# Two layer stacks on one core: SBUF tiles moved to multiples of 128 bytes, split weights 64 bytes past

## Chip, cores and metric

The kernel runs on one core of one Trainium2 chip. The time is that of one execution on the device in microseconds (us). Three timed runs of the kernel before have a median of 1580.65 us (1580.19 to 1584.49).

## What is computed

256 tokens of width 1024 pass through two layers and then a second block. Everything is float32.

```python
for i in range(2):                       # layers
    ff = swiglu(rms_norm(h, g[0]), w_gate_up[i, 0], w_down[i, 0]); h = h + 0.5 * rms_norm(ff, g[1])
    mix = short_conv_mixer(...) if i == 0 else gated_deltanet_mixer(...)   # on rms_norm(h, g[2])
    h = h + rms_norm(mix, g[3])
    ff = swiglu(rms_norm(h, g[4]), w_gate_up[i, 1], w_down[i, 1]); h = h + 0.5 * rms_norm(ff, g[5])
# second block: attention (three branches) beside an RWKV mixer, merged, and a convolved gated FFN
```

By far the most arithmetic is in the weight matrices: each of the four SwiGLUs multiplies by 1024 x 5632 and 2816 x 1024, the mixers by input and output projections, and the second block by the like. The recurrences, scores and norms are small beside them.

## The kernel before

**Weights.** All weight matrices are cut into tiles of 128 x 128 and laid in one stream (`wstream`) in the order of use, four tiles to a chunk of 128 x 512 floats. `Streamer` (line 620) brings each chunk by a DMA on the sync queue into one of six buffers `wraw`. ScalarE copies it, rounded, to a tile `whi` of type fp32r, and VectorE writes the difference `wraw - whi` to `wlo`; there are seven buffers of each. Twelve chunks are split ahead into room in the region `arG`.

**Products.** A weight product has 128 rows, 128 columns and 256 tokens. Its moving operand is split in the same way: `xh` and `xl` (1024 columns of the model in eight tiles of 256 tokens) for the up and input projections, tiles in the regions `a0`, `a1`, `a2` (all printed as `a`) for the down and output projections. `mm3` (line 794) issues three instructions for a tile: whi by the high part, whi by the low part, wlo by the high part. They sum into the same 256 columns of a PSUM bank. `mm3s` (line 801) does the same for a group of six column tiles, in the first two row tiles of a stage; on the first row tile it also multiplies by `x0`, the split update of the first tile (printed as `x`). The output of a column tile is complete after 8 row tiles (up) or 22 (down). Then VectorE and ScalarE take it from the bank.

**Order.** `Pace` (line 260) keeps an account of rough prices, makes a graph of all instructions and gives each engine a fixed order. It knows an operand by its tile's name and by the columns within the tile. Where in SBUF the tile lies isn't part of the account.

**Places.** Tiles are laid one behind another in each partition in the order of the calls `pool.tile`, each rounded up to 32 bytes. Before: `par` (2656 bytes), `con` (5888), `h`, `xh`, `xl`, `arM`, `fg`, `rb`, `rb2`, `acc` (all whole multiples of 128 long), `eps` (32), `half` (128), `tmp`, `stm` (whole multiples), five `pad` (1056 each), `x0`, `wraw`, `whi`, `wlo`, and then the regions `a0`, `a1`, `a2`, `arG`. The first starts at a multiple of 128. By these sums the starts modulo 128 bytes are:

| tiles | before | after |
|---|---|---|
| par | 0 | 0 |
| con, h, xh, xl, arM, fg, rb, rb2, acc | 96 | 0 |
| tmp, stm | 0 | 0 |
| pad0 to pad4 | 0, 32, 64, 96, 0 | 0, 32, 64, 96, 0 |
| x0 | 32 | 0 |
| wraw, whi, wlo | 32 | 64 |
| a0, a1, a2, arG | 32 | 0 |

Tiles inside these (the eight of xh, the four of a chunk, the slots of a) lie at whole multiples of 512 or 1024 bytes from the start.

The three products of a tile (lines 795 to 799):

```python
wh, wl = self.W.next()
nc.tensor.matmul(out, wh, xh, start=start, stop=False)
nc.tensor.matmul(out, wh, xl, start=False, stop=False)
nc.tensor.matmul(out, wl, xh, start=False, stop=stop)
```

Of the kernel before, what the change touches and what calls it, by code (L numbers as in the profile page):

```python
# [11 lines left out]
F32 = mybir.dt.float32  # L12
# [5 lines left out]
PSUM = bass.MemoryType.PSUM  # L18
# [28 lines left out]
class Product:  # L47
    """Tiles of one weight matrix in the order in which the tensor engine takes them: column tiles in
    groups, a group of several row tile by row tile, the columns beyond the groups one by one.
    A column tile is (weight, index, column ranges, row ranges of each row tile)."""  # L50
# [24 lines left out]
# The rule's input projection by column tile: queries 0-7, keys 8-15, values 16-31, output gates 32-47, and 48 for beta  # L75
# and the decay. The keys come first, whose inverse takes longest.
# [77 lines left out]
def low_rank(inputs):  # L154
    """The up projections of decay (with its bias as a row), learning rate and gate."""
    out = np.zeros((P, 1536), np.float32)
    out[:64, :512] = inputs["rwkv_w_up_2"][0]
    out[64, :512] = inputs["rwkv_w0_2"][0]
    out[64:, 512:1024] = inputs["rwkv_a_up_2"][0]
    out[:, 1024:] = inputs["rwkv_g_up_2"][0]  # L160
    return out


def cmp_w1(inputs):
    """Two tokens of a block, an even one and the next, over the partitions."""
# [4 lines left out]
def param_parts():  # L170
    """(name, columns, how the input is laid over 128 partitions)"""
# [66 lines left out]
class Staged:  # L238
    """Work on a sequence of items, whose later stages are issued with the next items' earlier ones."""
# [20 lines left out]
class Pace:  # L260
    """An account, by rough prices in us, of when each engine gets to what is issued to it and when each part of a
    tile was last written and read. Independent sequences of steps are interleaved by it."""
# [17 lines left out]
    def parts(self, ap):  # L280
        """The pieces of its tile that an access pattern touches."""
# [18 lines left out]
    def when(self, *aps):  # L300
        """When everything issued to these is done."""
# [20 lines left out]
    def columns(self, op, out, ins):  # L322
        """The columns for which a product holds the tensor engine, those that it counts, by its share of the rows, and
        the size of the square of the array that it takes."""
# [10 lines left out]
    def ranks(self):  # L335
        """Each instruction's place in the best of a few schedules. The first goes by the longest way to the end, and
        each other by the latest starts that the one before it leaves."""
# [27 lines left out]
    def schedule(self, order, before, after, forward):  # L365
        """Each instruction's start and end, where an engine that is free takes the first in this order of those that
        can start. The tensor engine runs at half its clock in a tick after one in which it was little used, and
        two products on the two halves of its columns go almost at once; so that it seldom is, products that use it
        little give way."""
# [76 lines left out]
    def arrange(self, tc, rank):  # L446
        """Has each engine take what was issued to it in the order of these ranks."""
# [8 lines left out]
    def node(self, engine, op, out, ins, outs, price):  # L456
        """An instruction of the graph, with those that come before it."""
# [132 lines left out]
class Chain:  # L590
    """A sequence of steps with the banks and buffers that it takes in turn."""
# [15 lines left out]
def alternate(*steps):  # L607
    """The sequences in turn, each waiting while another goes on."""
# [11 lines left out]
class Streamer:  # L620
    """Brings the weight tiles on chip ahead of their use, as high and low halves."""

    def __init__(self, K, n_raw=6, n_split=7):
        self.K = K
        self.nc = K.nc
        pool = K.pool
        self.raw = [pool.tile([P, CT * P], F32, name=f"wraw{i}") for i in range(n_raw)]
        self.hi = [pool.tile([P, ST * P], F32R, name=f"whi{i}") for i in range(n_split)]
        self.lo = [pool.tile([P, ST * P], F32R, name=f"wlo{i}") for i in range(n_split)]
# [1588 lines left out]
```

## Time and profile before

| what | value |
|---|---|
| median of three timed runs | 1580.65 us (1580.19 to 1584.49) |
| span of the profiled execution (its own time isn't recorded apart) | 1586.4 us |
| PE busy | 1569.7 us, 99%, 13,544 products |
| VectorE busy | 1202.2 us, 76% |
| ScalarE busy | 1026.9 us, 65% |
| DMA | 261.14 MB, mean 165 GB/s |

PE is TensorE's matrix product, PEld its loading of weights, DVE is VectorE, ACT is ScalarE, SP the sync queue. Every instruction of the program is issued through one helper, so all rows name the line L576, and they are told apart by the names of their tiles. A PE row's mean is the length of one product from start to end. As products are pipelined, the next one starts before the end, and the time from start to start is read from a timeline.

### The profile page before, as it was taken

How to read it: one execution, taken by the hardware profiler on the slowest of the kernel's cores; microseconds unless marked ns; L12 is line 12 of the kernel's file. 1: busy time of each engine (PE TensorE's matmuls, PEld its weight loads, DVE VectorE, ACT ScalarE, POOL GpSimd, SP SyncE). 2: the span in 40 equal slices, each digit the busy share in tenths (PEclk: the TensorE clock that was granted, in tenths of full speed). 3: DMA queues.
4: the chain of work that ended last, by engine and by line, in shares of the span. 5: the costliest groups of instructions: out<-in, count | busy, mean ns of one | idle time of the engine just before them, and what ended most of it. 6: DMA issues, size and time to landing. Idle time of an engine off the chain costs nothing.

```text
span 1586.4 us, 35927 instructions
## 1 busy us (share of the span) xinstructions
PE 1569.7 (99%) x13544; PEld 1517.6 (96%) x13544; DVE 1202.2 (76%) x2527; ACT 1026.9 (65%) x2153; POOL 10.4 (1%) x24
## 2 busy tenths in 40 slices
PE   9999999999999999999999999999999999999999
PEld 9999999999999999989898999999987877999999
DVE  7776597877658777689996778765887955889973
ACT  7555566765557557578887866555782766578763
POOL 0000000000000000000000000000010000000000
PEclk9999999999999999999999999999998989999999
DMA  8666556566665667525342456666533312566664
GB/s 275 192 186 187 180 176 186 170 190 187 184 185 167 201 193 245 180 79 168 116 138 81 135 159 201 187 187 184 168 106 101 120 35 87 172 187 188 187 194 118
DMA packets 142670, 261.14 MB, mean 165 GB/s; under 512 B 15904, under 2 KB 17952, under 8 KB 142368
## 3 DMA queue, kind: packets, MB, share of 16 engines
q1 hardware_dynamic: 142496, 258.84, 53.9%
q8 instruction: 106, 1.74, 0.4%
q14 instruction: 68, 0.56, 0.1%
HBM read 257.73 MB, written 1.05 MB: 163 GB/s over the span
## 4 chain that ended last, share of the span: by engine, by line
PE 93%; DVE 3%; ACT 2%; issue 1%; DMA 0%; SPq 0%; DVEq 0%
PE bank L576 93%; DVE a L576 1%; ACT a L576 1%; DVE wlo L576 1%; ACT stm L576 1%; DMA wraw<-wstream 0%; DVE arG L576 0%; ACT whi L576 0%; DVE stm L576 0%; ACT arG L576 0%; DVE fg L576 0%; DVE xl L576 0%; DVE tmp L576 0%; DVE acc L576 0%; ACT pad L576 0%
## 5 line engine op out<-in xcount | busy, mean ns | idle before, releaser
L576 ACT ACTIVATE whi<-wraw 128x512 fp32r<-128x512 f32 x956 | 599.3, 630 | 440.9 <-PE bank L576 335.5
L576 DVE TENSOR_TENSOR wlo<-wraw,whi 128x512 fp32r<-128x512 f32 x956 | 653.0, 688 | 291.2 <-ACT whi L576 282.6
L576 PE MATMUL bank<-xh,whi 128*128 128x256 f32 x2688 | 753.1, 284 | 6.1 <-DVE stm L576 3.6
L576 PE MATMUL bank<-xh,wlo 128*128 128x256 f32 x2688 | 751.6, 284 | 0.0
L576 PE MATMUL bank<-xl,whi 128*128 128x256 f32 x2688 | 745.7, 282 | 0.7 <-DVE xl L576 0.7
L576 PEld LDWEIGHTS bank<-xh,whi 128*128 128x128 f32 x2688 | 507.6, 190 | 15.2 <-issue 6.0
L576 PEld LDWEIGHTS bank<-xl,whi 128*128 128x128 f32 x2688 | 504.1, 189 | 8.8 <-issue 6.6
L576 PEld LDWEIGHTS bank<-xh,wlo 128*128 128x128 f32 x2688 | 502.0, 189 | 6.9 <-issue 6.0
L576 PE MATMUL bank<-a,whi 128*128 128x256 f32 x2272 | 411.0, 283 | 0.2
L576 PEld LDWEIGHTS bank<-a,whi 128*128 128x128 f32 x2272 | 353.6, 191 | 1.2 <-DVE a L576 0.4
L576 PE MATMUL bank<-a,wlo 128*128 128x256 f32 x1136 | 321.6, 283 | 0.0
L576 PEld LDWEIGHTS bank<-a,wlo 128*128 128x128 f32 x1136 | 217.2, 191 | 0.0
L576 DVE TENSOR_TENSOR tmp<-bank,rb 128x256 f32<-128x256 f32 x176 | 66.3, 418 | 8.0 <-ACT rb L576 0.6
L576 PE MATMUL bank<-a 64*128 64x256 f32 (+3 forms) x192 | 41.4, 397 | 1.4 <-DVE arG L576 1.4
L576 ACT ACTIVATE xh<-h,par 128x256 fp32r<-128x256 f32 x70 | 34.0, 498 | 12.0 <-DVE h L576 9.9
L576 ACT ACTIVATE arG<-bank 128x256 f32<-128x256 f32 (+2 forms) x87 | 37.8, 443 | 5.2 <-PE bank L576 4.9
L576 DVE SCALAR_TENSOR_TENSOR arG<-arG,par 128x256 f32<-128x256 f32 x88 | 40.0, 477 | 0.0
L576 ACT ACTIVATE a<-tmp 128x256 fp32r<-128x256 f32 x88 | 35.7, 406 | 6.5 <-DVE tmp L576 6.3
L576 DVE TENSOR_TENSOR acc<-acc,tmp 128x256 f32<-128x256 f32 x92 | 38.4, 418 | 2.0 <-ACT acc L576 0.9
L576 DVE TENSOR_TENSOR a<-tmp,a 128x256 fp32r<-128x256 f32 x88 | 36.7, 417 | 3.8 <-ACT a L576 3.8
L576 ACT ACTIVATE tmp<-tmp 128x256 f32<-128x256 f32 x88 | 35.4, 407 | 3.8 <-DVE tmp L576 3.7
L576 DVE TENSOR_TENSOR tmp<-tmp,tmp 128x256 f32<-128x256 f32 x88 | 36.7, 417 | 0.0
(253 smaller groups left out, 1229.5 us busy)
## 6 DMA issues: line engine op xcount, KB each, us to landing
wraw<-wstream SPq DMA_DIRECT2D x968, 256.0 KB, 2.8
arG<-cmp_w SPq DMA_DIRECT2D x1, 1024.0 KB, 4.7
out_dram<-h SPq DMA_DIRECT2D x8, 128.0 KB, 2.7
con<-consts SPq DMA_DIRECT2D x1, 734.0 KB, 4.7
h<-xt SPq DMA_DIRECT2D x1, 512.0 KB, 6.5
a<-lowrank SPq DMA_DIRECT2D x1, 512.0 KB, 4.0
par<-params SPq DMA_DIRECT2D x1, 283.5 KB, 4.8
h<-xt SPq DMA_DIRECT2D x2, 128.0 KB, 3.4
```

What stands on the lines that cost most here:

```text
L576: i = f(*args, **kw)
```

## The change

Only places change: the tiles `eps`, `half` and `pad` are allocated earlier, four filler tiles that nothing reads are added, and comments are gone. The sizes of the fillers (24, 32, 16 and 16 floats) bring the starts to the right column of the table above. No instruction, operand or order is changed.

```diff
 class Streamer:
     def __init__(self, K, n_raw=6, n_split=7):
         pool = K.pool
+        self.fill0 = pool.tile([P, 16], F32, name="fill2")
         self.raw = [pool.tile([P, CT * P], F32, name=f"wraw{i}") for i in range(n_raw)]
         self.hi = [pool.tile([P, ST * P], F32R, name=f"whi{i}") for i in range(n_split)]
         self.lo = [pool.tile([P, ST * P], F32R, name=f"wlo{i}") for i in range(n_split)]
+        self.fill1 = pool.tile([P, 16], F32, name="fill3")
...
+FILL = 24, 32
...
         self.par = pool.tile([P, N_PARAM], F32, name="par")
+        self.eps = pool.tile([P, 1], F32, name="eps")
+        self.half = pool.tile([P, 4, KD], F32, name="half")
+        self.pad = [pool.tile([P, T + 3], F32, name=f"pad{i}") for i in range(5)]
+        self.fill = [pool.tile([P, FILL[0]], F32, name="fill0")]
         self.con = pool.tile([P, N_CONST], F32, name="con")
+        self.fill += [pool.tile([P, FILL[1]], F32, name="fill1")]
         self.h = pool.tile([P, KD, T], F32, name="h")
...
-        self.eps = pool.tile([P, 1], F32, name="eps")
-        self.half = pool.tile([P, 4, KD], F32, name="half")
         self.tmp = [pool.tile([P, T], F32, name=f"tmp{i}") for i in range(8)]
         self.stm = [pool.tile([P, 512], F32, name=f"stm{i}") for i in range(4)]
-        self.pad = [pool.tile([P, T + 3], F32, name=f"pad{i}") for i in range(5)]
```

## Rows read from the trace of the kernel before

**Rows 1.** The page: busy time of each engine, and the chain that ended last.
```profile
PE 1569.7 (99%) x13544; PEld 1517.6 (96%) x13544; DVE 1202.2 (76%) x2527; ACT 1026.9 (65%) x2153; POOL 10.4 (1%) x24
...
PE 93%; DVE 3%; ACT 2%; issue 1%; DMA 0%; SPq 0%; DVEq 0%
```

**Rows 2.** The page's costliest groups: out<-in, shapes, count | busy, mean ns | idle before.
```profile
L576 ACT ACTIVATE whi<-wraw 128x512 fp32r<-128x512 f32 x956 | 599.3, 630 | 440.9 <-PE bank L576 335.5
```

**Rows 3.** Groups of PE by form, whole span; moving operand first, then weights.
```profile
L576 PE MATMUL bank<-xh,whi 128*128 128x256 f32 x2688 | 753.1, 284 | 6.1 <-DVE stm L576 3.6 <-DVE pad L576 1.3 <-ACT whi L576 0.6
...
L576 PE MATMUL bank<-a,whi 128*128 128x256 f32 x2272 | 411.0, 283 | 0.2
L576 PE MATMUL bank<-a,wlo 128*128 128x256 f32 x1136 | 321.6, 283 | 0.0
...
L576 PE MATMUL bank<-xh,arG 128*128 128x256 f32 x96 | 16.5, 284 | 0.0
...
L576 PE MATMUL bank<-x,whi 128*128 128x256 f32 x60 | 8.8, 283 | 0.0
...
L576 PE MATMUL bank<-x,arG 128*128 128x256 f32 x18 | 2.3, 283 | 0.0
```

**Rows 4.** Timeline of PE, first up projection: start us, length us, instruction, count.
```profile
59.76 0.28 PE L576 MATMUL bank<-xh,whi 128*128 128x256 f32 x1
...
61.41 0.28 PE L576 MATMUL bank<-xh,wlo 128*128 128x256 f32 x1
```

**Rows 5.** Timeline of PE, first up projection of the second layer, same operands.
```profile
549.75 0.28 PE L576 MATMUL bank<-xh,whi 128*128 128x256 f32 x1
...
551.45 0.28 PE L576 MATMUL bank<-xh,whi 128*128 128x256 f32 x1
```

**Rows 6.** Timeline of PE, first down projection.
```profile
149.74 0.28 PE L576 MATMUL bank<-a,wlo 128*128 128x256 f32 x1
...
151.18 0.28 PE L576 MATMUL bank<-a,wlo 128*128 128x256 f32 x1
```

**Rows 7.** Timeline of PE, the start of an up projection's first group.
```profile
932.19 0.87 PE L576 MATMUL bank<-xh,wlo 128*128 128x256 f32 x6
...
933.60 0.88 PE L576 MATMUL bank<-x,whi 128*128 128x256 f32 x6
...
935.04 0.64 PE L576 MATMUL bank<-x,whi 128*128 128x256 f32 x4
```

**Rows 8.** Timeline of PE, plain fp32 products in two places.
```profile
1182.76 0.27 PE L576 MATMUL bank<-con,a 128*128 128x128 f32 x1
...
1183.11 0.93 PE L576 MATMUL bank<-con,a 128*128 128x128 f32 x7
...
857.01 2.62 PE L576 MATMUL bank<-arG,a 128*128 128x128 f32 x22
```

**Rows 9.** Stretches: length, busy us (count) of each engine, granted clock, DMA share, GB/s.
```profile
26.00:130.00 104.00, 104.00 (x885) 103.97 (x884) 79.03 (x161) 62.62 (x121) 0.00 (x0) 1.00 0.65 196
131.00:193.00 62.00, 62.00 (x519) 62.00 (x518) 32.73 (x53) 33.95 (x62) 0.00 (x0) 1.00 0.62 185
503.00:600.00 97.00, 97.00 (x857) 96.92 (x856) 76.71 (x156) 59.86 (x116) 0.00 (x0) 1.00 0.67 196
700.00:900.00 200.00, 192.66 (x1859) 181.70 (x1859) 176.82 (x400) 165.29 (x389) 0.00 (x0) 0.99 0.40 123
1410.00:1518.00 108.00, 108.00 (x919) 108.00 (x919) 104.08 (x223) 87.78 (x202) 0.00 (x0) 1.00 0.63 186
```

**Rows 10.** Groups of VectorE and of ScalarE by form, whole span.
```profile
L576 DVE TENSOR_TENSOR acc<-acc,tmp 128x256 f32<-128x256 f32 x92 | 38.4, 418 | 2.0 <-ACT acc L576 0.9 <-ACT tmp L576 0.5
...
L576 DVE TENSOR_TENSOR tmp<-tmp,tmp 128x256 f32<-128x256 f32 x88 | 36.7, 417 | 0.0
...
L576 ACT ACTIVATE a<-tmp 128x256 fp32r<-128x256 f32 x88 | 35.7, 406 | 6.5 <-DVE tmp L576 6.3
L576 ACT ACTIVATE tmp<-tmp 128x256 f32<-128x256 f32 x88 | 35.4, 407 | 3.8 <-DVE tmp L576 3.7
```

## The prediction

> **What bounds the kernel now.** I read the page first: TensorE (PE) is busy 99% of the span in all forty slices, and the chain that ended last is 93% PE [rows 1]. The other engines have slack as a mean: VectorE 76%, ScalarE 65%. ScalarE's largest group waits 335.5 of its 440.9 idle us for PE, so weights are split ahead of their use and DMA isn't late [rows 2]. So the time is the number of matrix products times their pitch (start to start), and the pitch is what to look at. The 284 ns of one product in the groups is its pipelined length, not its pitch.
>
> The groups give the counts of weight products, all 128x256. With xh or xl moving there are three groups of 2688 (xh by whi, xh by wlo, xl by whi; the first is shown) and 96 + half as many whose weights lie in arG: 8208. With a there are 2272 + 1136 = 3408, with x0 (printed as x) 60, half as many by wlo, and 18 in arG: 108 [rows 3]. That is 11,724 of PE's 13,544 products.
>
> The timeline of PE then shows three pitches. At 59.76 to 61.41 fourteen intervals take 1.65 us: 117.8 ns [rows 4]. At 549.75 to 551.45, the same operands and the same instructions, fifteen intervals take 1.70 us: 113.3 [rows 5]. At 149.74 to 151.18, with a moving, twelve take 1.44 us: 120.0 [rows 6]. In columns at 2.4 GHz (the clock is 1.00 in these stretches, [rows 9]) these are 282.7, 272 and 288; 272 is 17 x 16 and 288 is 18 x 16, and 16 columns of four bytes are 64 bytes. A product has 256 columns, 16 such pieces. So I read one piece too many in the best state, two with a, and something between (17 2/3) in the xh state that fills most stages.
>
> **What the operands' places have to do with it.** Tile sizes and order in the code give each tile's place modulo 128 bytes (each rounded up to 32): xh, xl at 96; a, x0, arG, wraw, whi, wlo at 32. So a and x0 start at distance 0 from the weights, xh and xl at distance 64, and every one lies 32 past a multiple of 64. The best test is where only the moving operand changes: in one group of six column tiles, the same weights in the same buffers take 1.41 us for twelve products with xh and xl (117.5 each), and 1.44 for the next twelve, with x0 (120.0) [rows 7]. Distance 0 costs the full second piece, as with a; distance 64 sometimes nothing. Plain fp32 products (two passes each of half rate) point the same way: seven products con,a (96 and 32, distance 64) take 0.93 us, and less the length of one (0.27) that is 110 each; 22 products arG,a (both 32) take 2.62, less 0.27, 111.9 each [rows 8].
>
> **The change part by part.** (1) No instruction is added, removed or moved: only places change, and the planner goes by tile names and offsets inside tiles. (2) Weights go to 64 past a multiple of 128, all moving operands to 0: distance 64 for a and x0 too, so the collision that made 288 should go. (3) All start at a multiple of 64: 1024 bytes then lie in 16 pieces instead of 17, so the first extra piece should go as well. [...] The nearest row for a pair that doesn't collide is con,a: 110 by two-digit rows for 256 column times, so 107 to 110; I take 109.2 (262 columns). [...]
>
> The sum, against the profiled span of 1586.4:
> - a and x0: 3516 x (120.0 - 109.2) = 38.0 us.
> - xh, xl in the 117.8 state: the window 26:130 has 885 products, some 2.4 of which straddle its edges: 104 us at 117.8. Five windows are of this kind (26:130, 218:262, 310:414, 953:1056, 1410:1518; the first and the last are shown), 463 us together, so 3930 products x 8.6 = 33.8 us [rows 9].
> - xh, xl in the 113.3 state: 503:600 and 1374:1408 (the first is shown), 131 us, 1156 products x 4.1 = 4.7 us [rows 9].
> - the other 3122 of xh, xl lie in first groups and in the two mixers (700:900, 1125:1340), at either pitch or slower; priced at 4.1 each, 12.8 us.
> Together 89.3 us, if PE stays the bound.
>
> What is late next. In 1410:1518 VectorE is busy 104.08 of 108 us [rows 9]; PE alone would come to 100.0, so VectorE stops it near 104.6: 4.6 us back. In the mixers the products wait on chains of small steps (in 700:900 VectorE 176.82 of 200, PE 192.66): I let half of the 12.8 fall, 6.4 us. Elsewhere the cover holds: in 26:130 VectorE needs 79 us where PE will need 96; in 131:193, 33 of 56. The DMA share of 26:130, 0.65, would become 0.70 [rows 9].
>
> VectorE and ScalarE themselves I cost at nothing: a tensor-tensor step of 128x256 takes 417 ns with every operand at 0 (tmp) and 418 with acc at 96; ScalarE takes 407 from tmp to tmp and 406 from tmp to a [rows 10]. The spread of 1 ns over the 956 splits on each engine is 1 us either way, and lies beside PE. On the other side of the account, constants (con) now move from distance 64 to distance 0 against a and arG: about 2 ns more per such product (111.9 against 110). If all 1820 plain products paid 2.3 that is 4.2 us, if all gained it -4.2; one run of seven is shown [rows 8], and these pairs are a small part of the 1820, so I take +0.5.
>
> 89.3 - 11.0 - 0.5 = 77.8 us, span 1508.6. The three timed runs have their median, 1580.65, at 0.9964 of the profiled span (only the span is known of that execution), so the time is 1503.
>
> **The rivals.**
> *A. Distance works, the start doesn't.* The seventeenth piece stays, as a rounding of 262 columns up to the next 16. Then a and x0 join the two states of xh: all at 113.3 gives 3516 x 6.7 + 3930 x 4.5 = 41.2 us, less some 3 for VectorE, time 1542; all of a at 117.8 and xh as now gives 7.7 us, 1573. For it: no weight product of today starts at a multiple of 64, so the gain of the start rests on the number 272 alone. Against: con,a is under 272 columns though both ends are off by 32. [...]
> *B. The start works, but collisions stay at distance 64,* as they now do in five of seven long xh stretches: the step from 113.3 to 117.8 (4.4 ns) remains on top of 109.2, so 113.6 or less. a and x0 3516 x 6.4 = 22.5, slow xh 3930 x 4.2 = 16.5, the rest 10: about 49 us, less 4, time 1536; with the short state in half of the stretches 1520.
> *C. Nothing.* Pitch would be made by something else that only goes with the phase, and time stays 1580.65. The two pitches of the same operands in rows 4 and 5 speak for it, rows 7 against. [...]
> *D. Slower.* What spares xh the second piece today is not its distance but its own start at 96, or the odd count of 17 pieces, which shifts the phase at each product; with even counts of 16 and common starts each product meets the weights of the next in the same piece. xh then falls into a's 120.0, and a stays: 3930 x 2.2 + 1156 x 6.7 + half of 3122 x 6.7 = 27 us more, time 1607. It decides as soon as more than some two thirds of xh's products leave 113 to 118 for 120 or over while a gains nothing.
>
> **How the numbers follow.** The forecast, 1490 to 1515 by 1 to 2 ns of pitch and by the whole or none of the 11 us that VectorE takes back, gets 0.50; B (1515 to 1542) 0.18; A (1540 to 1573) 0.17; C 0.07; D 0.08. Lowest, at 106.7 and with nothing lost, the span would be 1467. Faster by over 0.3% (what a measurement of this kernel tells from no change) is 0.50 + 0.18 + 0.17 = 0.85, within 0.07, slower 0.08. The range 1486 to 1572 leaves out C, D and the far ends of the forecast and A, 0.18. For the forecast alone it is 1490 to 1515.
>
> **What would show it.** After: the timeline in the a stages at 109 instead of 120 shows parts 2 and 3; 113.3 everywhere shows A; 109 in some stretches and 111 to 114 in others shows B; 120 with xh shows D. VectorE's share in the last up projection (1410:1518) should be near 100%, and its 417 ns unchanged. The forecast is wrong if a's pitch stays above 112, or if PE falls and waits of equal size appear for VectorE or DMA in stages where I counted on cover.

## The result, and the profile after

The changed kernel takes 1557.65 us (median of 4 runs, 1553.3 to 1564.22), the kernel before 1580.42 on the same chip (1580.16 to 1584.49): a ratio of 0.9845 [0.9815, 0.9875]. It is faster by 1.55%, where 4.9% were forecast; the time lies in the range, between the two ends of rival A (1542 and 1573). The four runs of the changed kernel spread over 10.9 us. An estimated 6 us of that (0.004 of the span) go with the granted clock, whose mean was 0.993 in the slowest run, the one profiled, and 0.997 in the three others. What makes the rest isn't shown, as only one execution was profiled.

The page of the changed kernel has the busy times and the chain that answer to [rows 1], and the ScalarE group that answers to [rows 2]:

```profile
span 1562.0 us, 35927 instructions
...
PE 1545.8 (99%) x13544; PEld 1495.5 (96%) x13544; DVE 1199.4 (77%) x2527; ACT 1026.1 (66%) x2153; POOL 10.4 (1%) x24
...
PE 95%; ACT 2%; DVE 1%; issue 0%; DMA 0%; SPq 0%; DVEq 0%; ACTq 0%
...
L576 ACT ACTIVATE whi<-wraw 128x512 fp32r<-128x512 f32 x956 | 599.2, 631 | 416.9 <-PE bank L576 311.8
```

The counts are the old ones, PE is still the bound, and its busy time fell by 23.9 us with the span's 24.4. So the pitch changed; the timeline of PE says by how much. Columns: start us, length us, instruction, count. It answers to [rows 4], [rows 6], and, in the second pair of xh, to an up projection of the second layer:

```profile
59.77 0.28 PE L576 MATMUL bank<-xl,whi 128*128 128x256 f32 x1
...
61.58 0.28 PE L576 MATMUL bank<-xh,wlo 128*128 128x256 f32 x1
...
149.79 0.28 PE L576 MATMUL bank<-a,wlo 128*128 128x256 f32 x1
...
150.85 0.28 PE L576 MATMUL bank<-a,wlo 128*128 128x256 f32 x1
...
959.76 0.28 PE L576 MATMUL bank<-xh,wlo 128*128 128x256 f32 x1
...
961.53 0.28 PE L576 MATMUL bank<-xh,wlo 128*128 128x256 f32 x1
```

Sixteen intervals in 1.81 us are 113 ns; with a, nine in 1.06 us are 117.8; in the last pair fifteen in 1.77 are 118. Nothing runs at 109. The windows (stretch: length, busy us and count of PE, weight loads, VectorE, ScalarE, GpSimd, granted clock, DMA share, GB/s), beside [rows 9], show it over whole stages:

```profile
28.00:126.00 98.00, 98.00 (x867) 98.00 (x866) 76.78 (x157) 60.38 (x118) 0.00 (x0) 1.00 0.69 199
129.00:190.00 61.00, 61.00 (x520) 61.00 (x520) 32.81 (x52) 33.59 (x61) 0.00 (x0) 1.00 0.64 187
490.00:588.00 98.00, 98.00 (x867) 98.00 (x866) 76.70 (x156) 60.44 (x118) 0.00 (x0) 1.00 0.68 199
943.00:1045.00 102.00, 102.00 (x868) 102.00 (x867) 77.33 (x157) 60.72 (x117) 0.00 (x0) 1.00 0.65 189
685.00:885.00 200.00, 192.77 (x1853) 181.54 (x1852) 176.48 (x402) 166.51 (x394) 0.00 (x0) 0.98 0.40 122
1391.00:1495.00 104.00, 104.00 (x920) 104.00 (x919) 101.56 (x222) 86.89 (x202) 0.00 (x0) 1.00 0.66 194
```

867 products take 98 us in the first and third stretch, and 868 of the same kind take 102 in the fourth: two pitches of one code, as in rows 4 and 5, but now the quick one prevails. Averaged start to start over whole stretches, three of the long xh stretches that had 117.8 before run at 113.36 and so does the short one at 212.8; the one at 942 keeps 117.8. All of a is at 117.78, from 120.0.

That accounts for the span: 884 + 406 + 884 + 934 = 3108 products of xh and xl gained 4.4 ns, 13.7 us; 3408 of a gained 2.2, 7.5; 272 in the mixer at 685 to 885 gained 4.4, 1.2; x0 some 0.5. Two first groups that went from 113.4 to 117.8, and 162 products with weights in arG (113.5 to 118.7; these weights now lie 0 modulo 128 from xh), cost some 2.1. That is 20.8 of 24.4 us. The other 3.6 needn't come from the change: between the last down projection of the layers and the second block's own weight products the same work took 236.7 us before and 230.8 after, and the mean granted clock there was 0.94 in the one execution and 0.97 in the other. At the full clock the products of xh and xl in it, waits included, took 137.5 ns from start to start before and 137.2 after:

```profile
1121.00:1357.70 236.70, 232.75 (x2028) 195.19 (x2027) 182.20 (x432) 153.13 (x361) 9.08 (x18) 0.94 0.32 100
```

```profile
1108.20:1339.00 230.80, 226.70 (x2030) 190.65 (x2028) 182.04 (x432) 153.07 (x361) 9.08 (x18) 0.97 0.34 103
```

### The profile page after: what moved, and what is told of

Its sections match the earlier page's. It is cut to its first block, busy times and chain, and to the rows that moved or that the text cites. A ratio compares the mean times of both kernels' runs of the same rounds, so it can differ in the third digit from the quotient of the medians.

```text
span 1562.0 us, 35927 instructions
## 1 busy us (share of the span) xinstructions
PE 1545.8 (99%) x13544; PEld 1495.5 (96%) x13544; DVE 1199.4 (77%) x2527; ACT 1026.1 (66%) x2153; POOL 10.4 (1%) x24
## 4 chain that ended last, share of the span: by engine, by line
PE 95%; ACT 2%; DVE 1%; issue 0%; DMA 0%; SPq 0%; DVEq 0%; ACTq 0%
PE bank L576 95%; ACT a L576 1%; ACT stm L576 1%; DVE a L576 0%; ACT arG L576 0%; ACT whi L576 0%; DVE fg L576 0%; DVE arG L576 0%; DMA h<-xt 0%; DVE wlo L576 0%; DVE xl L576 0%; DVE pad L576 0%; DVE tmp L576 0%; ACT pad L576 0%; ACT arM L576 0%
## 5 line engine op out<-in xcount | busy, mean ns | idle before, releaser
L576 PE MATMUL bank<-a,whi 128*128 128x256 f32 x2272 | 403.8, 280 | 0.2
L576 PEld LDWEIGHTS bank<-a,whi 128*128 128x128 f32 x2272 | 347.1, 188 | 1.2 <-DVE a L576 0.5
L576 PE MATMUL bank<-a,wlo 128*128 128x256 f32 x1136 | 317.4, 279 | 0.0
L576 PEld LDWEIGHTS bank<-a,wlo 128*128 128x128 f32 x1136 | 212.7, 187 | 0.0
```

The source lines that it names most:

```text
L576: i = f(*args, **kw)
```

## The experiments

Two things were to be told apart first: whether the start or the distance made the gain, and where the floor of a product lies. "Distance" is how far the weights lie past the moving operand, in bytes. At first it was counted modulo 128. Later runs show that it has to be counted modulo 256, and where that changes the reading the value modulo 256 is given too. A pair such as (32, 96) is the place of the moving operand and that of the weights.

**The floor, by itself.** PE alone, no network: stretches of 256-column products that alternate as xh by whi, xh by wlo, xl by whi, each with other places; then other column counts, all at distance 64.

```diff
+for d in (0, 16, 32, 48, 64, 80, 96, 112):
+    SEGMENTS.append((0, d, 256, 128, "triple", 192))   # moving at, weights at, columns, weight columns
...
+for n in (128, 192, 240, 244, 248, 252, 256, 320, 384, 512):
+    SEGMENTS.append((0, 64, n, 128, "triple", 96))
```

> A stream of nothing but weight products on PE, in segments of 96 or 192, with no other engine at work: eight distances between moving operand and weights (0 to 112 bytes modulo 128, moving at 0), four places at equal distance with other starts, ten column counts at distance 64, half as many weight columns, one tile again and again, and distance 64 four times. The network itself is left out. Theory 'distance' (pitch goes by the distance modulo 128 and by a phase, the start itself counts for nothing): at 256 columns 120.0 ns at distance 0, 113.3 or 117.8 at 64, the same for (32, 96), (96, 32) and (64, 0), and 120.0 again for (32, 32). The 272 columns of the best pitch would be 262 rounded up to the next 16: then 240, 244 and 248 columns go at 106.7 ns and 252 and 256 at 113.3. Rival 'fixed extra' (always 16 columns over the width): 240 at 106.7, 244 at 108.3, 248 at 110.0, 252 at 111.7. Rival 'start': (0, 64) below 113.3 here, where no other engine disturbs, and (32, 96) above it. Rival 'other engines': with VectorE and ScalarE silent every segment of 256 columns goes at 109.2.

Windows of this kernel (as above, without VectorE, which does nothing here): distance 64, then (32, 96), (96, 32), (64, 0) and (32, 32); then 128 and 252 columns:

```profile
106.00:126.00 20.00, 20.00 (x179) 20.00 (x178) 0.00 (x0) 0.00 (x0) 1.00 0.00 1
...
196.00:216.00 20.00, 20.00 (x179) 20.00 (x178) 0.00 (x0) 0.00 (x0) 1.00 0.00 1
218.00:238.00 20.00, 20.00 (x179) 20.00 (x178) 0.00 (x0) 0.00 (x0) 1.00 0.01 2
240.00:260.00 20.00, 20.00 (x172) 20.00 (x171) 0.00 (x0) 0.00 (x0) 1.00 0.00 1
262.00:282.00 20.00, 20.00 (x169) 20.00 (x169) 0.00 (x0) 0.00 (x0) 1.00 0.01 2
285.00:294.00 9.00, 9.00 (x83) 9.00 (x83) 0.00 (x0) 0.00 (x0) 1.00 0.01 2
...
340.00:349.00 9.00, 9.00 (x78) 9.00 (x77) 0.00 (x0) 0.00 (x0) 1.00 0.00 0
```

Start to start: 120.0 at distance 0, whether both lie at 0 or at 32; 113.3 at 64; and 117 to 120 at the six distances between. (64, 0) and (96, 32) have one distance, 192 modulo 256, and yet the first ran at 117.8 and the second, behind the quick stretch at (32, 96), at 113.3. With no other engine at work and both starts on multiples of 64 the floor is 113.3 (272 columns' time, at the 0.416 ns a column that the next run on PE alone shows), the same as at (32, 96). So the start saves nothing. The counts of columns say why neither a rounding nor a fixed addition fits: 128, 192 and 240 columns take 111.7 to 112.0, 252 take 120.0, 256 take 113.3, 512 take 233.3. Up to 240 something that doesn't depend on the columns sets the pace.

**The start, in the kernel.** Everything 32 bytes further, all distances kept.

```diff
-FILL = 24, 32
+FILL = 32, 32
```

> The changed kernel with every operand 32 bytes further: moving operands at 32, weights at 96 modulo 128, so the distance of 64 stays and every start lies 32 past a multiple of 64, as before the change. Theory 'distance': a at 117.8 ns, xh at 113.3 or 117.8, time as the changed kernel, 1550 to 1566. Rival 'start' (the multiples of 64 are what keeps xh at 113.3 in most stages now): xh falls back to 117.8 in most stages, a at 117.8 or more, time 1570 to 1576.

1558.09 us, ratio 0.9854 [0.9815, 0.9893], against 0.9845 of the change itself. No operand of the weight products is on a multiple of 64 any more and nothing is lost: the start counts for nothing. In this kernel's windows even the up projection that stayed slow after the change is quick (532 products in 60 us):

```profile
30.00:120.00 90.00, 90.00 (x796) 90.00 (x796) 70.73 (x145) 54.84 (x108) 0.00 (x0) 1.00 0.69 198
135.00:185.00 50.00, 50.00 (x427) 50.00 (x426) 26.37 (x42) 27.39 (x51) 0.00 (x0) 1.00 0.66 187
965.00:1025.00 60.00, 60.00 (x532) 60.00 (x531) 45.23 (x89) 34.70 (x67) 0.00 (x0) 1.00 0.70 194
```

**The distance, in the kernel, from both sides.** First the changed kernel with its weights on a multiple of 128 too (distance 0 modulo 128 for all); then the kernel before with its weights alone 64 further (0 from xh, 64 from a). Modulo 256 the distance is 128 for all in the first, and 128 from xh and 192 from a in the second.

```diff
-        self.fill0 = pool.tile([P, 16], F32, name="fill2")
+        self.fill0 = pool.tile([P, 32], F32, name="fill2")
...
-        self.fill1 = pool.tile([P, 16], F32, name="fill3")
+        self.fill1 = pool.tile([P, 32], F32, name="fill3")
```

> The changed kernel with the weights at 0 modulo 128 too, so every operand starts at a multiple of 128 and the distance is 0 everywhere. Theory 'distance': all weight products at 120.0 ns, xh too, so 8208 products lose 4 to 7 ns and the time is 1595 to 1615, slower than the kernel before. Rival 'start': with all starts on multiples of 64 the pitch stays at 113 to 118 and the time at 1553 to 1575.

```diff
+        self.fill0 = pool.tile([P, 16], F32, name="fill2")
...
         self.lo = [pool.tile([P, ST * P], F32R, name=f"wlo{i}") for i in range(n_split)]
+        self.fill1 = pool.tile([P, 16], F32, name="fill3")
```

> The kernel before with the weights alone moved by 64 bytes: xh, xl and the weights at 96, a, x0 and arG at 32. The distances are swapped (xh 0, a 64), nothing else moves and no start becomes a multiple of 64. Theory 'distance': a from 120.0 to 117.8 or 113.3, xh from 113.3 to 117.8 up to 120.0; 3408 products gain 2.2 to 6.7 ns and 8208 lose 3.8 on average, time 1590 to 1605. Rival 'tile' (a is slow for what it is, its regions or its order of products, not for its place): a stays at 120.0, xh keeps its two pitches, time 1575 to 1585.

1601.51 us, ratio 1.012 [1.0078, 1.0162], and 1602.76, ratio 1.0111 [1.0074, 1.0149]: slower than before both times. The first two windows of the first kernel:

```profile
30.00:120.00 90.00, 90.00 (x761) 90.00 (x760) 67.61 (x138) 52.70 (x103) 0.00 (x0) 1.00 0.66 187
135.00:185.00 50.00, 50.00 (x424) 50.00 (x423) 26.73 (x42) 27.08 (x50) 0.00 (x0) 1.00 0.67 186
```

Start to start xh is at 118.67 in both kernels; a is at 118.67 in the first and 117.78 in the second. So 0 modulo 128 is what costs, for either operand, and 64 modulo 128 is worth 2.2 ns only to a (120.0 before). Why a doesn't reach the 113.3 of xh there was open.

**What sets the floor, and what changes the state.** PE alone again: 32, 64 and 128 weight columns by 128, 256 and 512 columns; distances of 64 more than multiples of 128; and, in a stretch that runs at 117.8, one odd product, that is, one unlike its neighbours.

```diff
+for m in (32, 64, 128):
+    for d in (0, 64):
+        for n in (128, 256, 512):
+            SEGMENTS.append((0, d, n, m, "triple", 72))
...
+for odd in ((0, 64, 32, 128), (0, 64, 64, 128), (0, 64, 96, 128), (0, 64, 128, 128), (0, 64, 192, 128), (0, 64, 320, 128), (0, 64, 512, 128),
+            (0, 64, 256, 32), (0, 64, 256, 64), (0, 0, 256, 128), (0, 32, 256, 128), (0, 96, 256, 128), "plain", "plain256"):
```

> Weight products on PE alone again; the network is left out. Two questions. First, what sets the floor of 272 columns: products of 128, 256 and 512 columns with 32, 64 and 128 weight columns, at distance 0 and 64. Theory 'load' (a load of 128 weight columns takes some 268 columns' time whatever streams, since 128 and 192 columns went at 111.7 ns in the sweep): with 32 weight columns, 128 columns go near 55 to 60 ns, 256 at 107 to 110 and 512 at 214 to 216, and distance counts little. Rival 'stream' (the moving operand itself can't be read faster than 17 pieces for 256 columns): 256 stay at 113.3 with 32 weight columns, and 512 at 226 to 233. Second, what chooses 113.3 or 117.8 at distance 64: after 48 products at distance 0 come 48 at distance 64 (117.8 in the sweep), then one odd product, then 72 at distance 64. Theory 'phase': the pitch holds until an odd product shifts the load against the stream, and some odd products, the plain fp32 one among them, bring 113.3. Rival 'far bits' (which pieces further on meet): odd products change nothing, and the distances 192, 320, 448, 576, 1088 differ among one another in a way that repeats. Distances 0, 128 and 512 are alike, 118 to 120, if only the value modulo 128 counts.

The timeline: 128, 256 and 512 columns with 32 weight columns, then 128 columns with 128 weight columns. A row's length is its intervals and once the length of the last product (0.22 us in the first row, 0.28 in the second and the fourth, 0.39 in the third):

```profile
26.80 1.42 PE L65 MATMUL bank<-x,w 128*32 128x128 f32 x21
...
32.78 1.41 PE L65 MATMUL bank<-x,w 128*32 128x256 f32 x11
...
44.70 2.48 PE L65 MATMUL bank<-x,w 128*32 128x512 f32 x10
...
144.75 2.51 PE L65 MATMUL bank<-x,w 128*128 128x128 f32 x21
```

(1.42 - 0.22) / 20 = 60 ns for 128 columns, 113 for 256, and 231 start to start for 512. From 128 to 256 columns the pitch grows by 53.3 ns (60.0 to 113.3), 0.416 ns or 1/2.4 ns a column; at that rate, by which the prediction counts columns, the three are 144, 272 and some 554 columns' time. With only 32 weight columns to load, at distance 0 as at 64, the stream alone has this floor; the load of 128 weight columns is the other one, 111.7 ns, when 128 columns are streamed. At 128 columns the distance makes no difference (60.0 with 32 or 64 weight columns, 111.7 with 128, at 0 as at 64). With 128 weight columns 256 columns take 120.0 at distance 0 and 113.3 at 64; but 512 columns take 226.8 at 0 and 233.3 at 64, so 64 isn't best for every length. With 64 weight columns 256 columns took 113.3 in the sweep and 116.7 (at 0) to 119 (at 64) here.

The distances of 64 more than multiples of 128 (192, 320, 448 and more), run one behind the other after a quick stretch, all held 113.3; 0 and 512 took 120.0, and 128 took 118.7. The window at distance 192:

```profile
220.50:230.20 9.70, 9.70 (x88) 9.70 (x87) 0.00 (x0) 0.00 (x0) 1.00 0.00 0
```

A stretch at 117.8 stays there by itself. An odd product of 128 columns, one with 32 weight columns, or a plain fp32 one throws it to 113.3; those of 32, 64, 96, 192, 320 or 512 columns don't, nor one with 64 weight columns or at distance 0, 32 or 96. So one set of operands has two steady pitches, and what ran before decides between them.

**Where in SBUF.** The same stretches with the moving operand below and above the weights, and with a's pattern of steps.

```diff
+        for kb in (0, 8, 16, 24, 32, 40, 48, 56):
+            SEGMENTS.append((tl, kb, 0, 64, "x", kick, 72))    # tl: "low" or "high"
```

> Weight products on PE alone, weights near 104 KB of the partition as in the full kernel, moving operands in eight places below them (28 to 84 KB) and eight above (124 to 180 KB), always at distance 64; the network is left out. Each stretch of 72 starts with one odd product, first a plain fp32 one, then one of 128 columns. It asks why a holds 117.8 in every stage of the changed kernel, even straight after xh at 113.3, though both lie at 0 and the weights at 64. Theory 'place': what matters beside the distance modulo 128 is on which side or in which large part of SBUF the moving operand lies; all high places give 117.8 (or another pitch than the low ones) whatever the odd product before them. Rival 'pattern': a's high and low parts lie 22 KB apart and run through 22 tiles; the 'a' pattern gives 117.8 in the low place too and the 'x' pattern 113.3 in the high one. Rival 'lottery': both pitches occur in both places. The stretches at (0, 64), (64, 0), (32, 96), (96, 32) and (0, 0) after the same odd product tell whether it counts which of the two lies 64 ahead; by theory 'distance' the first four are alike.

The part with the odd product of 128 columns tells, in this kernel's timeline:

```profile
302.75 8.70 PE L66 MATMUL bank<-low,w 128*128 128x256 f32 x72
311.29 0.22 PE L54 MATMUL bank<-low,w 128*128 128x128 f32 x1
311.35 8.40 PE L66 MATMUL bank<-low,w 128*128 128x256 f32 x72
```

Stretch by stretch it throws the pitch over, 117.8, 113.3, 117.8, in both places. The exception is the stretch at (32, 96) behind one at (64, 0), which stayed at 117.8 in both places. With a's pattern the low place shows the quick pitch and the high one, thrown over next, the slow one. So neither the place in KB nor the pattern by itself holds a at 117.8; the next distances show a's pattern at 113.3 in the high place too. Most of the plain products ran ahead of their stretches (three stood in their place), so that half tells little but that 117.8 lasts.

**The mirror.** Moving operands at 64, weights on a multiple of 128, in the whole kernel.

```diff
-FILL = 24, 32
+FILL = 24, 48
```

> The changed kernel with the 64 bytes on the other side: moving operands at 64, weights at 0 modulo 128 (constants at 0). All starts are multiples of 64 and the distance is 64, as in the changed kernel. Theory 'distance alone': time as the changed kernel, 1550 to 1566, xh at 113.3 in most stages. Theory 'side' (which of the two is 64 ahead chooses the pitch after the plain product that ends each first group; before the change the moving operand lay in the upper half, now the weights do): xh falls back to 117.8 in most stages, a stays at 117.8, time 1568 to 1578.

1574.95 us, ratio 0.9954 [0.9928, 0.9979], in between. Of its seven long stretches of xh three hold 113.36 and four 117.78; the windows of two:

```profile
30.00:120.00 90.00, 90.00 (x767) 90.00 (x766) 68.33 (x141) 53.92 (x104) 0.00 (x0) 1.00 0.68 190
320.00:400.00 80.00, 80.00 (x708) 80.00 (x708) 62.93 (x127) 47.92 (x93) 0.00 (x0) 1.00 0.70 196
```

Stretches with the same distance choose differently within one execution, so distance isn't the whole rule for xh. Modulo 256 the distances here are those of the changed kernel, 64 for xh and 192 for a; but con lies 64 past acc and the other operands of that region, and in the changed kernel 128.

**a's stages rebuilt, and the odd product put into the kernel.** PE alone with the places modulo 1024 and the order of an up and a down projection; and the changed kernel with one product of 128 columns ahead of the fourth row tile in seven stages of a.

```diff
+    def kick(self, x):
+        w, (i, j) = self.W, divmod(self.W.pos, ST)
+        self.nc.tensor.matmul(self.banks[7][:, :P], w.at[i][0][:, j * P:(j + 1) * P], x[:, :P], start=True, stop=True)
...
+                if g == 0 and k == 3 and key in KICKED:
+                    self.kick(x(c, k)[0])
```

> Weight products on PE alone, in the addresses and the order of an up and a down stage of the changed kernel (moving operands at 0, a ring of fourteen weight tiles at 64, a first group of six column tiles, the plain product of 256 after it, column tiles one by one, then a's pattern of 22 + 22 tiles above the weights); the network is left out. Between up and down stands nothing, an odd product of 128 columns ('kick'), the a pattern below the weights, or the up pattern above them. Theory 'phase' (two stable states, toggled by an odd product, kept otherwise): without a kick the down stretch keeps the pitch of the up stretch before it; a kick turns 113.3 into 117.8 or back, in a's pattern too. Rival 'a is different' (its pattern above the weights can't hold 113.3, since it is at 117.8 in all seven stages of the changed kernel): down stays at 117.8 even after up at 113.3 and after either kick.

> The changed kernel with one odd weight product of 128 columns, into the free bank 7, before the fourth row tile of each of the seven stages whose moving operand is a (four down stages, sc_out, gdn_out, cdown). Nothing reads it. Theory 'phase': the seven stages turn from 117.8 to 113.3 at the kick and stay there; some 3300 products gain 4.4 ns, 14.7 us, the kicks cost 0.15 each, so the time is some 13 us under the changed kernel's, 1541 to 1548. Rival 'a is different': the kicks change no pitch and cost 1 us, time 1553 to 1566.

In the first everything runs at 117.8 and stays there whatever odd product stands between. The second takes 1555.65 us, ratio 0.9835 [0.9782, 0.9888], not told apart from the change; a stays at 117.78. Both rebuilt places have the weights 64 bytes *short* of the moving operand (at 64 where it lies at 128, modulo 256; a distance of 192), the sweep had them 64 past. That pointed to the sign.

**The sign.** PE alone, distances 64 to 960 in steps of 128, each stretch after nothing, after an odd product of 128 columns, and after one with 32 weight columns.

```diff
+    for d in (64, 192, 320, 448, 576, 704, 832, 960):
+        for kick in (None, (128, 128), (128, 128), (256, 32), (128, 128)):
+            SEGMENTS.append((tl, d, "x" if tl == "low" else "a", kick, 60))
```

> Weight products on PE alone at eight distances of the weights past the moving operand, 64 to 960 bytes modulo 1024, all 64 modulo 128, in two places and two patterns, five stretches of 60 each: one without and four with an odd product before it (of 128 columns, or with 32 weight columns). The network is left out. In the changed kernel xh has the distance 64 and goes at 113.3 in most stages, a has -64 = 960 and goes at 117.8 in all. Theory 'order' (64 ahead and 64 behind aren't alike, because the pieces are shared by more than two): at some distances, 64 among them, odd products bring 113.3, at 960 and 448 they never do. Rival 'lottery': each distance shows both pitches in equal parts over its four odd products.

The timeline at distance 192:

```profile
66.05 7.28 PE L58 MATMUL bank<-low,w 128*128 128x256 f32 x60
73.17 0.22 PE L45 MATMUL bank<-low,w 128*128 128x128 f32 x1
73.23 7.28 PE L58 MATMUL bank<-low,w 128*128 128x256 f32 x60
80.35 0.28 PE L45 MATMUL bank<-low,w 128*32 128x256 f32 x1
80.47 6.96 PE L58 MATMUL bank<-low,w 128*128 128x256 f32 x60
```

After an odd product of 128 columns a stretch is at 117.8 each time; only the one with 32 weight columns frees it (6.68 us in 59 intervals, 113.2). 448, 704 and 960 behave as 192; 64, 320, 576 and 832 run at 113.3 at once, and there the odd product of 128 columns throws the pitch back and forth. So the period is 256 bytes over these eight distances, and modulo 256 the change has a at 192. This doesn't make 192 slow in itself: the sweep's (96, 32), the window at 192 above and the last row here held 113.3. Both pitches last at 64 and at 192; what differs is which of them is left behind an interruption. Behind an odd product of 128 columns 192 (and 448, 704, 960) came out at 117.8 in all 24 cases of this run.

**The sign, in the kernel.** The changed kernel, with the last filler behind the weights 384 or 256 bytes longer: a0 to a2 and arG, which lie behind it, move; xh does not. Distance modulo 256 for a: 64 in the first, 192 as before in the second.

```diff
-        self.fill1 = pool.tile([P, 16], F32, name="fill3")
+        self.fill1 = pool.tile([P, 112], F32, name="fill3")      # the second kernel: 80
```

> The changed kernel with the regions a0 to a2 and arG 384 bytes further (a filler of 112 floats in place of 16 behind the weights): they still start at a multiple of 128, but the weights now lie 64 past them modulo 512, as they do against xh, and not 64 short of them. Theory 'order': a goes at 113.3 in most of its seven stages, 3400 products gain 4.4 ns, time 1540 to 1548. Rival 'a is different' or 'modulo 128 alone': a stays at 117.8, time 1553 to 1566.

> The same with a0 to a2 and arG 256 bytes further (a filler of 80 floats): the weights lie 192 past a modulo 512. Theory 'order' in the form that only 64 short (-64 modulo 512) is bad: a at 113.3, 1540 to 1548. In the form that only 64 past is good, or 'modulo 128 alone': 117.8, 1553 to 1566.

1541.75 us (1540.9 to 1545.48), ratio 0.9751 [0.9722, 0.9781], and 1563.74, ratio 0.9885 [0.9853, 0.9918]. The ten runs of the second lie between 1552.62 and 1576.41, those at a granted clock of 0.988 at the upper end. 128 bytes between the two kernels decide a's pitch. The stage of a, first the one, then the other:

```profile
135.00:185.00 50.00, 50.00 (x443) 50.00 (x442) 27.44 (x43) 28.15 (x52) 0.00 (x0) 1.00 0.69 198
```

```profile
135.00:185.00 50.00, 50.00 (x427) 50.00 (x426) 26.80 (x42) 26.98 (x50) 0.00 (x0) 1.00 0.66 189
```

Start to start 113.33 against 117.78, in all stages of a; 3408 x 4.4 ns are 15.2 us, and by its ratio (0.9751 against 0.9845) the first is some 15 us faster than the change. It beats both kernels.

**What holds xh at 117.8.** In the kernel before xh had distance 64 and still ran slow. PE alone: eight places of the moving operand modulo 256, weights always 64 past, after odd products and after plain ones whose own distance is 0, 64, 128 or 192.

```diff
+for p in range(0, 256, 32):
+    for kick in (None, (128, 128), (128, 128), (256, 32), "plain 0", "plain 64", "plain 128", "plain 192", "plain 0"):
+        SEGMENTS.append(("low", p, 64, kick, 60))
```

> Weight products on PE alone, moving operand at eight places modulo 256 (0 to 224 in steps of 32), weights always 64 past it; before each stretch of 60 nothing, a product of 128 columns (twice), one with 32 weight columns, or a plain fp32 product whose stationary operand lies 0, 64, 128 or 192 past its moving one modulo 256. The network is left out. Theory 'side': with the moving operand at 64, 96, 192, 224 (upper half of a 128-byte unit) stretches take 117.8 after odd products that give 113.3 at 0, 32, 128, 160. Theory 'plain product': the pitch after a plain product goes by that product's own distance or by the pitch before it, the same in all eight places. Rival 'lottery': no order in either.

An odd product with 32 weight columns brought 113.3 in every place, but plain ones left one pitch or the other, with no rule by the place (at place 0 and 224 always the quick one, elsewhere mixed). By their own distance there is a hint: those whose stationary operand lay 128 past the moving one left the pitch as it had been in seven of eight places; those at 0, 64 and 192 turned it over in 14 of 32. So plain products can choose the pitch of the stretch behind them. In the kernel six of the seven long stretches of xh follow straight behind a plain product of the constants, con, with acc as its moving operand. In the kernel before, with the products around it (one plain product leaves two records, hence x2):

```profile
25.53 0.28 PE L576 MATMUL bank<-xl,whi 128*128 128x256 f32 x1
25.65 0.59 PE L576 MATMUL bank<-acc,con 128*128 128x256 f32 x2
25.89 0.47 PE L576 MATMUL bank<-xh,wlo 128*128 128x256 f32 x1
```

So con was moved: alone in the changed kernel (back to 96 past a multiple of 128), and by 64 in the mirror.

```diff
-FILL = 24, 32
+FILL = 48, 8      # the mirror: 40, 32 in place of 24, 48
```

> The changed kernel with the constants alone moved, from 0 to 96 modulo 128 (fillers of 48 and 8 floats in place of 24 and 32); xh, weights and a lie as in the changed kernel. con is the stationary operand of the plain product after each first group. Theory 'side': xh stays at 113.3 in all or all but one of its long stretches, a at 117.8, time 1551 to 1565. Theory 'plain product': several long xh stretches turn to 117.8, time 1562 to 1578.

> The mirrored kernel (moving operands at 64, weights at 0 modulo 128) with the constants moved to 64 too, so that con lies 128 past acc modulo 256, as in the changed kernel. Theory 'side': about half of the long xh stretches stay at 117.8, time 1568 to 1584 as in the mirrored kernel. Theory 'plain product': xh at 113.3 in all or all but one of the long stretches, time 1551 to 1565.

1559.49 us (two runs), ratio 0.9827 [0.9774, 0.988]; and 1554.94 (two runs), ratio 0.9798 [0.9737, 0.9859], against the mirror's 0.9954 [0.9928, 0.9979]. All of xh is at 113.36 in both, a at 117.78. The first row is the same window as the mirror's:

```profile
30.00:120.00 90.00, 90.00 (x796) 90.00 (x795) 70.65 (x143) 54.17 (x106) 0.00 (x0) 1.00 0.67 196
```

In the mirror con's new place turned four slow stretches quick; in the changed kernel it does no harm at the old place modulo 128. So it isn't con's own place that counts, but where it lies to the others.

**The gain, rebuilt from the kernel before.** First con alone 128 bytes further (128 before and 128 behind, so all else keeps its place modulo 256); then also a0 to a2 and arG 192 further, so that the weights lie 64 past a. xh and the weights stay where they were.

```diff
+        self.fill0 = pool.tile([P, 32], F32, name="fill0")
         self.con = pool.tile([P, N_CONST], F32, name="con")
+        self.fill1 = pool.tile([P, 32], F32, name="fill1")
```

The second kernel has this as well:

```diff
         self.lo = [pool.tile([P, ST * P], F32R, name=f"wlo{i}") for i in range(n_split)]
+        self.fill1 = pool.tile([P, 48], F32, name="fill3")
```

> The kernel before with the constants alone moved, by 128 bytes (32 floats of filler before con and 32 after it; all else moves by 256 and so keeps its place modulo 256). con then lies 128 from acc modulo 256 instead of 0; weights, xh and a keep their places (32, 224, 32 modulo 256). Theory 'plain product': xh goes at 113.3 in all or nearly all long stretches, a stays at 120.0, time 1560 to 1568. Theory 'weights moved': nothing changes, xh at 117.8 in most stretches, time 1577 to 1588.

> The same and the regions a0 to a2 and arG 192 bytes further, so that the weights lie 64 past a modulo 256 as they do past xh. xh, a, weights and constants lie 32 or 96 past multiples of 128, none at a multiple of 64. Theory 'distance modulo 256 and plain product': all xh and a at 113.3, time 1539 to 1547, as the best kernel so far. Theory 'start after all': a above 113.3, time 1552 or more.

1564.5 us, ratio 0.9903 [0.9874, 0.9932], and 1543.26, ratio 0.9772 [0.9742, 0.9802]. First windows of the one, then of the other:

```profile
30.00:120.00 90.00, 90.00 (x797) 90.00 (x796) 70.39 (x144) 54.41 (x107) 0.00 (x0) 1.00 0.70 199
135.00:185.00 50.00, 50.00 (x419) 50.00 (x418) 26.19 (x41) 26.69 (x50) 0.00 (x0) 1.00 0.67 185
```

```profile
30.00:120.00 90.00, 90.00 (x796) 90.00 (x796) 71.10 (x146) 54.88 (x108) 0.00 (x0) 1.00 0.69 200
135.00:185.00 50.00, 50.00 (x444) 50.00 (x443) 27.46 (x43) 28.10 (x52) 0.00 (x0) 1.00 0.70 198
```

Moving con alone takes the long stretches of xh to 113.36 and leaves a at 120.0: this is the larger part of what the change gained. With a at 64 as well all is at 113.33, no operand of the weight products stands on a multiple of 64, and the time is that of the best kernel.

The profiled executions of all these kernels show together what the plain product acc,con does to the pitch. Compare the last products of the first group, ahead of it, with the stretch of xh behind it, six pairs in each kernel:

| con past acc, modulo 256 | kernels | pitch ahead, and behind |
|---|---|---|
| 0 | before | 113.3 ahead in all six; 117.8 behind in five |
| 64 | mirror | 113.3 turned to 117.8 twice; of four at 117.8 two turned to 113.3 |
| 128 | the change, and seven variants of it or of before with xh at distance 64 | the same ahead and behind in all 48 |
| 224 | the change with con alone moved | the same ahead and behind in all six |

So in the kernel before it is this product that threw quick stretches of xh into the slow pitch, and the change, by putting con 128 past acc, ended it. The one stretch of xh that stays slow after the change had been slow in its first group already (117.8 from 923.4 on): what made it so isn't shown.

## Why the prediction was wrong

The direction was right, and so was the reading that PE's pitch bounds the kernel. The size was not: 77.8 us were forecast and 22.8 came.

- **Part (1)** held: the instructions and their order on each engine are the old ones. VectorE and ScalarE cost nothing more (419 and 407 ns for the groups acc<-acc,tmp and a<-tmp, against 418 and 406 in [rows 10]), and the DMA share of the first up projection is 0.69, near the 0.70 that was forecast for it.
- **Part (3) is the step that failed**: "1024 bytes then lie in 16 pieces instead of 17, so the first extra piece should go as well". It stood in every term of the sum, 4.1 ns for each of 11,724 products. The start saves nothing (32 further: 0.9854 against 0.9845); 113.3 is the least that 256 columns took on PE alone, in every place tried, and with 32 weight columns too. No run shows the 109.2 (262 columns) that the sum uses, nor the 106.7 of its lowest span: both were the author's estimates, and the runs have 113.3 in their place. Reading 272 as 17 pieces of 16 columns rested on one number. The 144 columns' time that 128 columns take still fits it (nine pieces in place of eight), but 512 take some 554 and not 528, and moving the start changes nothing. The neighbour taken for the unknown pitch, the plain product con,a [rows 8], was the wrong one: it takes 110 ns for 128 columns, some two columns' time for each (by the lengths of records in the kernel before, 379 ns for 256 and 592 for 512 columns of stm,con, 0.83 ns a column), and that didn't carry over to a product that takes 113.3 for 256.
- **Part (2)** was half right: 0 modulo 128 is the costly distance (putting xh there, at 128 modulo 256, gives ratios of 1.012 and 1.0111), and taking a off it gained 7.5 us. But the sum had distance modulo 128, where it counts modulo 256: a was moved to 192, where all its stages run at 117.8, and at 64 they run at 113.3. At this point 15 us were left behind, which the version with the weights 64 past a picks up.
- **xh's gain** was counted under the start (33.8 us, of which 13.7 came). What came has another cause: the constants moved against acc, from 0 to 128 modulo 256, and the plain product acc,con ahead of each stretch no longer turns it slow. Of such products the prediction said only that con,a and arG,a would lose or gain a few ns each (0.5 us); that one of them chooses the pitch of the hundreds behind it wasn't seen. The two pitches of the same operands in rows 4 and 5 were the hint, and it was put under rival C.
- **What is late next** wasn't put to the test at 109. At 113.3 VectorE needs 101.56 of 104 us in the last up projection and PE is busy all of the 104: no wait took the gain.
- **Rivals.** A, "distance works, the start doesn't", is nearest to the result, and its price for "all at 113.3", 1542, is what the kernel with a at 64 takes, 1541.75. That is partly luck: the 3 us that it took off for VectorE didn't show, its reason for the floor (262 columns rounded up to the next 16) fails on the counts of columns (240 take 112.0 and not 106.7), and xh's gain came by con and not by distance. B never showed: no stretch ran at 109. C's mechanism (the phase, not the places) exists beside the places. D's falling back of xh is real at 0 modulo 128 (118.7 in place of D's 120) and gives 1601 to 1603, near its 1607; the change doesn't put xh there, and what it made of even and odd counts of pieces fell (alone on PE, distance 0 takes 120.0 at 0 and at 32 past). In the sweep the pitch went from 113.3 to 120.0 with PE alone at work and only places changed, so it takes no other engine to move it.

What stays open: why the plain product turns the pitch over with con 0 or 64 past acc, and not at 128 or 224. PE alone gave a hint for 128 and no more. Open too is what made the first group at 923 slow in the changed kernel's profile (a loss of some 4 us; with everything 32 further no long stretch was slow), and whether that differs from run to run.

## What to carry to other kernels

Before pricing a pitch below the lowest one in the trace, measure the instruction's own floor in a loop of nothing else: a number that factors nicely is no mechanism. Where products with fresh weights run back to back and load and stream take about as long (here 111.7 ns, the pitch of 128 columns with 128 weight columns, and 113.3, that of 256 columns with 32), put the weights 64 bytes past the moving operand modulo 256 (measured for 256 columns by 128 weight columns in fp32r; at 512 columns 64 was the slower of the two distances tried), and look in the timeline for stretches of the same code at two pitches: they are time that a layout, or a few products ahead of the stretch, can win back.

## What the runs showed of the hardware that had not been expected

- A product of 256 columns in fp32r took at least 113.3 ns, with 32, 64 and 128 weight columns; with 32 weight columns 128 take 60.0, so each of the 128 columns between costs 0.416 ns, and 512 take 227 to 233 over all.
- Products with 128 fresh weight columns, back to back, never went below 111.7 ns.
- 252 columns (120.0) were slower than 256 (113.3) at distance 64, in one stretch of each.
- Two pitches, 113.3 and 117.8, are each stable for hundreds of products with the same operands; one product of 128 columns between them throws the one into the other at distance 64, with four exceptions in the runs on PE alone, and never into the quick one at 192 (24 cases, with 448, 704 and 960).
- A plain fp32 product ahead of a stretch can turn its pitch over for all of its hundreds of products: with con 0 past acc it did so five times of six, with con 128 past acc never in 48.
